# Score products of an RWKV-7 layer: two heads in turn, chunk by chunk, into two PSUM banks

## The chip, the core and the metric

The kernel runs as one program on one core of a Trainium2 chip. The metric is the device time of one execution in microseconds (us). The core has five instruction streams that run side by side and meet at semaphores: TensorE (PE) for matrix products, VectorE (DVE), ScalarE (ACT) and GpSimd (POOL) for element-wise work, and SyncE (SP), which issues most of the DMAs. PE writes its results to PSUM, which has eight banks of 128 partitions by 512 fp32 values here; the other engines take them from there.

## The reference

Two decoder layers over one sequence of 256 tokens with model width 1024. Layer 0 mixes tokens by RWKV-7 (16 heads of 64), layer 1 by block attention; each mixer is followed by a SwiGLU feed-forward part, and each sub-layer by a residual and a LayerNorm. The part that matters here, for every head of layer 0:

```python
r, k, v = einsum(...)            # three projections of the shifted input
w = -softplus(-(w0 + tanh(xw @ w1) @ w2)) - 0.5
a = sigmoid(a0 + (xa @ a1) @ a2)
g = sigmoid(xg @ g1) @ g2        # the gate, applied at the end
...
# one state S (64 x 64) per head, carried over the tokens:
# decayed by exp(-exp(w)), corrected along the normalised key, fed with k and v, read with r
```

The kernel doesn't walk over the tokens one by one. It cuts the 256 tokens into four chunks of 64, computes inside each chunk all products of keys and receptances (the scores), masks them, inverts the triangular matrix that the correction gives, and carries the state only from chunk to chunk.

## The kernel before

Layer 0's mixer takes the first 236 us, its feed-forward part follows, then layer 1. Within the mixer the stages are these. Names are those of the tiles, as the rows show them.

- **Projections.** k, r and v; weights are split into a high and a low part (ACT casts `hi`, DVE or POOL subtracts to get `lo`). The v products are issued where the planner finds room.
- **Operands of the scores.** For each of four quads q (two pairs of heads each; index j is the pair, hp the head of a pair, which sits in partitions 0 to 63 or 64 to 127) `KB[q]` holds the scaled keys and `AR[q]` the correction vectors and receptances. Generators `weigh(q)` and `keys(q)` write `KB`; `weigh` has waits of the form `yield I.idle("DVE")`, so the planner lets it go on only when, by its model, DVE has little queued.
- **Scores** (`scores(q)`, the function of the change). For each pair and head four products of 64x128 by 128 columns, one per chunk, fill one bank `sc`. `done`, one DVE multiplication of the bank by the causal mask, writes it to `SC`. There are 16 banks in all.
- **Transposes of KB** (`bkt`), the `bonus` sums from `rk`, products of the gate (`g<-mix`, then `hg`, then `g<-hg`).
- **Inverse** (`inverse`). Four DVE transposes `LT`, 31 steps of multiply (`tmp`) and add (`TT`) on DVE, each waiting for the last one, two transposes `TN`, and four transposes back into `SC`. It starts when all four quads of `SC` are there.
- **Merge** (`merge`). Products of 32x32: four groups `n` (16 each), copied by ACT into `TN`, then four groups `t`, copied by ACT into `SC`.
- **Recurrence** (`recurrence`). For four chunks and two halves f of the heads: products `z`, `u`, `s`, `y`, with copies between them. Calls of `fill` between the steps let other products (v, then the output projection o) in.
- **Tail.** Transposes `yt`, normalisation and gate, output projection `o`, residual, LayerNorm (`xtok`), then the feed-forward part begins (`gn`, `gu`).

What sets the order of the instructions: the generators are handed to `Issue` with a rank (scores has 4, `done` has 0, lower goes first). `Issue.run` keeps a modelled clock for each engine (`Clock.charge`), always resumes the ready generator of lowest rank, and so fixes one order of instructions for each engine before the kernel runs. On the chip each engine follows its order strictly; an instruction that waits holds up everything behind it on that engine. All instructions are recorded under one line, L300, that of the helper that issues them, so the rows tell them apart by tile names alone.

In `scores` the planner gets control back at each `yield 0.0`, and at each `I.after` a `done` is registered that it may place as soon as the bank is modelled as ready:

```python
I.after(ps, done, j, hp, ps)
yield 0.0
```

Of the kernel before, what the change touches and what calls it, by code (L numbers as in the profile page):

```python
# [23 lines left out]
NC = T // C  # L24
# [5 lines left out]
HALF = (slice(0, 64), slice(64, 128))  # L30
# [392 lines left out]
def trunk(ctx, tc, a, out):  # L423
# [16 lines left out]
    def nm(s):  # L440
        uid[0] += 1
        return f"{s}{uid[0]}"

    def bank(name):
        return pp.tile([128, 512], F32, tag="ps", name=nm(name))

    def slot(shape, name, dtype=F32):
        return tp.tile([128] + shape, dtype, tag="t4", name=nm(name))
# [7 lines left out]
    I = Issue(clk)  # L456
    E = {}

    def ev(name):
        return E.setdefault(name, Event())  # L460
# [9 lines left out]
    def mm(ps, lhsT, rhs, start, stop, **kw):  # L470
        pe.matmul(ps, lhsT, rhs, start=start, stop=stop, **kw)
# [21 lines left out]
    for u in range(4):  # L493
        q, o = u // 2, (u % 2) * 2
# [35 lines left out]
    def count(n, fn):  # L530

        left = [n]

        def call():
            left[0] -= 1
            if left[0] == 0:
                fn()
        return call
# [231 lines left out]
    AR = [slot([2, NC, 2, C], "AR") for _ in range(4)]  # L770
# [68 lines left out]
    KB = [slot([2, NC, 2, C], "KB") for _ in range(4)]  # L839
# [36 lines left out]
    def scores(q):  # L876

        yield ev(f"kb{q}")
        yield ev(f"ar{q}")
        yield ev("SC")  # L880
        fin = count(4, lambda: I.reach(ev(f"sc{q}"), SC[:, :, q * 2:q * 2 + 2]))

        def done(j, hp, ps):
            dve.tensor_tensor(SC[:, hp, q * 2 + j], ps.rearrange("p (c t) -> p c t", c=NC),
                              mask[:, None, :].to_broadcast([128, NC, 128]), ALU.mult)
            fin()

        for j in range(2):
            for hp in range(2):
                rs = HALF[hp]  # L890
                ps = bank("sc")
                for c in range(NC):
                    mm(ps[:, c * 128:(c + 1) * 128], KB[q][rs, j, c].rearrange("p o t -> p (o t)"),
                       AR[q][rs, j, c].rearrange("p o t -> p (o t)"), True, True)
                I.after(ps, done, j, hp, ps)
                yield 0.0

    def transposed(q):

# [779 lines left out]
    for q in range(4):  # L1679
        I.add(2, keys(q), True)  # L1680
        I.add(4, scores(q))
        I.add(5, transposed(q))
# [92 lines left out]
```

## Time and profile before

| | |
|---|---|
| median of 3 runs | 750.04 us (747.36 to 753.28) |
| the profiled execution's own time | 746.08 us |
| its span, first to last instruction | 744.3 us |
| busy PE, DVE, ACT, POOL | 93%, 73%, 51%, 25% of the span |
| mean granted TensorE clock | 0.959 of full speed |
| mixer of layer 0 | 0 to 236 us |
| first score product, last score bank masked | 84.6 us, 102.3 us |
| steps of the inverse | 108.6 to 140.7 us |
| recurrence, first u to last y | 164.5 to 195.5 us |

The span is the time from the first to the last instruction of the profiled execution; 1.8 us of its own time lie outside. The profiled execution is one of the quicker ones: 4 us under the median. Shares of busy time are averages over the whole program: PE is the fullest engine over the span, but between 70 and 140 us it is DVE that has no gaps. The granted clock is the share of full speed at which TensorE was allowed to run in a stretch: 1.00 is its upper level of 2.4 GHz, 0.50 the lower one of 1.2 GHz.

### The profile page before, as it was taken

The page shows a single profiled execution, that of the slowest core. Times are in us where ns is not written, and L with a number is a line of the kernel's source. Part 1 is how long each engine was busy: PE and PEld are TensorE (multiplying, and loading weights), DVE is VectorE, ACT ScalarE, POOL GpSimd, SP SyncE. Part 2 cuts the span into 40 slices and gives each one's busy share as a digit, 9 for nine tenths or more (in the row PEclk, how much of TensorE's full clock was granted, in tenths as well). Part 3 has the DMA queues.
Part 4 walks back from the last instruction along what each step waited for, and adds up shares of the span by engine and source line. Part 5 has one row for each costly group of instructions (what it writes and reads, how often), then busy time and mean ns, then how long its engine had stood idle before and what let it go on. Part 6 is the DMA issues. An engine that isn't in the chain of part 4 may idle for free.

```text
span 744.3 us, 11759 instructions
## 1 busy us (share of the span) xinstructions
PE 689.4 (93%) x4500; PEld 587.6 (79%) x4500; DVE 539.7 (73%) x915; ACT 382.2 (51%) x679; POOL 185.0 (25%) x132
## 2 busy tenths in 40 slices
PE   6899795998889999999999699999979999999995
PEld 5799684777678888888888488777769888888885
DVE  7989999948897766656657935977776665666576
ACT  5974134456545554554556324756635545545550
POOL 5777964343463000000001613113040000000000
PEclk9999898779899999999999889999989999999999
DMA  6445312120565655655557615345046556555551
GB/s 242 152 147 187 107 57 86 57 83 7 188 223 172 227 178 190 196 183 187 197 182 240 201 34 182 125 142 199 28 170 195 178 194 197 175 194 192 187 160 56
DMA packets 33576, 117.21 MB, mean 157 GB/s; under 512 B 3808, under 2 KB 4832, under 8 KB 33520
## 3 DMA queue, kind: packets, MB, share of 16 engines
q1 hardware_dynamic: 31936, 110.89, 44.6%
q10 hardware_dynamic: 1584, 5.57, 2.5%
q8 instruction: 35, 0.57, 0.3%
q14 instruction: 21, 0.17, 0.1%
HBM read 115.40 MB, written 1.05 MB: 156 GB/s over the span
## 4 chain that ended last, share of the span: by engine, by line
PE 68%; DVE 8%; ACT 2%; DMA 2%; issue 1%; DVEq 0%; ACTq 0%
PE gu L300 29%; PE acc L300 14%; PE qkv L300 9%; PE o L300 5%; DVE xtok L300 3%; PE gn L300 2%; PE v L300 1%; PE tr L300 1%; DMA raw<-in_w_qkv_dram 1%; DVE sc L300 1%; PE ptr L300 1%; PE pv L300 1%; PE n L300 1%; ACT hi L300 1%; PE att L300 1%
## 5 line engine op out<-in xcount | busy, mean ns | idle before, releaser
L300 DVE TENSOR_TENSOR lo<-raw,hi 128x1024 fp32r<-128x1024 f32 (+1 forms) x172 | 210.3, 1228 | 144.6 <-ACT hi L300 144.4
L300 ACT CAST hi<-raw 128x1024 fp32r<-128x1024 f32 (+1 forms) x214 | 212.0, 999 | 186.2 <-issue 93.1
L300 PE MATMUL gu<-xw,hi 128*128 128x512 f32 x640 | 226.1, 395 | 0.0
L300 PE MATMUL gu<-xw,lo 128*128 128x256 f32 x640 | 179.8, 281 | 0.0
L300 POOL TENSOR_TENSOR lo<-raw,hi 128x1024 fp32r<-128x1024 f32 (+1 forms) x41 | 87.8, 2158 | 261.3 <-ACT hi L300 257.6
L300 PEld LDWEIGHTS gu<-xw,hi 128*128 128x128 f32 x640 | 120.3, 188 | 27.1
L300 PEld LDWEIGHTS gu<-xw,lo 128*128 128x128 f32 x640 | 120.9, 189 | 0.7
L300 PE MATMUL acc<-hi,hl 128*128 128x512 f32 (+1 forms) x180 | 53.8, 369 | 0.0
L300 PE MATMUL acc<-lo,hh 128*128 128x512 f32 (+1 forms) x180 | 53.7, 368 | 0.0
L300 PE MATMUL acc<-hi,hh 128*128 128x512 f32 (+1 forms) x180 | 53.5, 366 | 0.0
L300 PE MATMUL qkv<-hi,xhi 128*128 128x512 f32 x96 | 40.7, 424 | 2.3 <-ACT xhi L300 2.3
L300 PE MATMUL qkv<-hi,xlo 128*128 128x512 f32 x96 | 39.3, 409 | 0.0
L300 ACT ACTIVATE silu<-silu 128x256 f32<-128x256 f32 x40 | 16.7, 417 | 44.0 <-DVE silu L300 44.0
L300 PE MATMUL qkv<-lo,xhi 128*128 128x512 f32 x96 | 39.0, 406 | 0.0
L300 PEld LDWEIGHTS acc<-hi,hl 128*128 128x128 f32 x180 | 32.8, 188 | 6.2
L300 PEld LDWEIGHTS acc<-lo,hh 128*128 128x128 f32 x180 | 32.7, 188 | 5.6
L300 PEld LDWEIGHTS acc<-hi,hh 128*128 128x128 f32 x180 | 31.8, 188 | 6.0
L300 PE MATMUL o<-hi,xhi 128*128 128x512 f32 x64 | 28.6, 447 | 3.0 <-ACT xhi L300 3.0
L300 PE MATMUL o<-lo,xhi 128*128 128x512 f32 x64 | 27.5, 430 | 0.0
L300 PE MATMUL o<-hi,xlo 128*128 128x512 f32 x64 | 27.3, 429 | 0.0
L300 POOL TENSOR_TENSOR ro<-ro 128x512 f32<-128x512 f32 x8 | 12.1, 1515 | 57.1 <-DVE ro L300 57.1
L300 PE MATMUL gn<-hi,xw 128*128 128x256 f32 x128 | 24.4, 287 | 0.4 <-ACT xw L300 0.3
(227 smaller groups left out, 1292.5 us busy)
## 6 DMA issues: line engine op xcount, KB each, us to landing
raw<-in_w_in_dram SPq DMA_DIRECT2D x80, 512.0 KB, 3.3
raw<-in_w_dn_dram SPq DMA_DIRECT2D x44, 512.0 KB, 3.3
raw<-in_w_qkv_dram SPq DMA_DIRECT2D x24, 512.0 KB, 3.4
raw<-in_w_o_dram SPq DMA_DIRECT2D x20, 512.0 KB, 3.5
raw<-in_w_r_dram SPq DMA_DIRECT2D x8, 512.0 KB, 3.4
raw<-in_w_v_dram SPq DMA_DIRECT2D x8, 512.0 KB, 3.3
raw<-in_w_if_dram SPq DMA_DIRECT2D x8, 512.0 KB, 3.6
raw<-in_w_k_dram SPq DMA_DIRECT2D x6, 512.0 KB, 3.8
```

What stands on the lines that cost most here:

```text
L300: ins = f(*args, **kw).ins
```

## The change

The two heads of a pair get a bank each at once. The products are then issued chunk by chunk, head 0 and head 1 in turn, so that neighbouring products read different halves of the partitions and write different banks. Both `done` calls are registered when the pair's eight products are issued, and the generator gives control back to the planner once for each pair, not once for each head. The arithmetic, the number of products and the number of banks are as before.

```diff
         for j in range(2):
+            ps = [bank("sc") for _ in HALF]
+            for c in range(NC):
+                for hp, rs in enumerate(HALF):
+                    mm(ps[hp][:, c * 128:(c + 1) * 128], KB[q][rs, j, c].rearrange("p o t -> p (o t)"),
+                       AR[q][rs, j, c].rearrange("p o t -> p (o t)"), True, True)
             for hp in range(2):
-                rs = HALF[hp]
-                ps = bank("sc")
-                for c in range(NC):
-                    mm(ps[:, c * 128:(c + 1) * 128], KB[q][rs, j, c].rearrange("p o t -> p (o t)"),
-                       AR[q][rs, j, c].rearrange("p o t -> p (o t)"), True, True)
-                I.after(ps, done, j, hp, ps)
-                yield 0.0
+                I.after(ps[hp], done, j, hp, ps[hp])
+            yield 0.0
```

Since the planner gets control back at other points of its modelled clock, the order of the other work moves too, on PE, DVE, ACT and POOL, from the scores up to the start of the feed-forward part. SP's order stays the same. Three places follow; numbers behind the names are buffers and differ between the two programs.

**PE, around the scores of the last quad (q = 3).** `sc` are score products, `bkt` transposes of KB, `v` products of the value projection; KB_133 and AR_123 are the operands of quad 3. Before:

```order
L300 MATMUL sc_1025<-AR_122,KB_132 128x128 x4
L300 MATMUL bkt_1033<-cst,KB_130 128x128 x4
...
L300 MATMUL bkt_1069<-cst,KB_132 128x128 x4
L300 MATMUL sc_1075<-AR_123,KB_133 128x128 x4
L300 MATMUL sc_1081<-AR_123,KB_133 128x128 x4
L300 MATMUL sc_1087<-AR_123,KB_133 128x128 x4
L300 MATMUL sc_1093<-AR_123,KB_133 128x128 x4
L300 MATMUL bonus_169<-selrk,rk_1023 128x2 x4
L300 MATMUL v_1106<-hi_831,xhi_865 128x512
```

With the change:

```order
L300 MATMUL sc_1013<-AR_122,KB_132 128x128
L300 MATMUL bkt_1026<-cst,KB_130 128x128 x4
...
L300 MATMUL bkt_1058<-cst,KB_132 128x128 x4
L300 MATMUL v_1067<-hi_831,xhi_865 128x512
L300 MATMUL v_1067<-lo_832,xhi_865 128x512
...
L300 MATMUL bonus_169<-selrk,rk_1108 128x2 x4
...
L300 MATMUL v_1068<-hi_912,xlo_868 128x512
L300 MATMUL sc_1151<-AR_123,KB_133 128x128
L300 MATMUL sc_1152<-AR_123,KB_133 128x128
```

Between the last `bkt` of quad 2 and the first `sc` of quad 3 there now stand 36 v products and all four bonus groups; before there stood nothing. The other 12 v products of this half follow the scores.

**DVE, from the operands of the scores to the inverse.** The rows of DVE's order, before:

```order
L300 TENSOR_TENSOR AR_122<-r_799,G_114 128x8x64
L300 TENSOR_TENSOR KB_133<-k_117,E_112 64x8x64 x2
L300 TENSOR_TENSOR KB_133<-kkr_119,a_110 64x8x64
L300 TENSOR_TENSOR AR_123<-r_869,G_114 128x8x64
L300 TENSOR_TENSOR SC<-sc_945,cst 128x512
L300 TENSOR_TENSOR rk_1045<-r_701,k_116 128x512
...
L300 TENSOR_TENSOR SC<-sc_1087,cst 128x512
L300 STREAM_TRANSPOSE LT_165<-SC 32x32x32
L300 TENSOR_TENSOR SC<-sc_1093,cst 128x512
L300 STREAM_TRANSPOSE LT_165<-SC 32x32x32 x3
```

With the change:

```order
L300 TENSOR_TENSOR rk_1102<-r_799,k_117 128x512
L300 TENSOR_TENSOR AR_123<-r_869,G_114 128x8x64
L300 TENSOR_TENSOR rk_1108<-r_869,k_117 128x512
L300 TENSOR_TENSOR SC<-sc_945,cst 128x512
...
L300 TENSOR_TENSOR SC<-sc_1013,cst 128x512
L300 TENSOR_TENSOR KB_133<-k_117,E_112 64x8x64 x2
L300 TENSOR_TENSOR KB_133<-kkr_119,a_110 64x8x64
L300 TENSOR_TENSOR SC<-sc_1151,cst 128x512
L300 TENSOR_TENSOR SC<-sc_1152,cst 128x512
L300 TENSOR_TENSOR SC<-sc_1162,cst 128x512
L300 TENSOR_TENSOR SC<-sc_1163,cst 128x512
L300 STREAM_TRANSPOSE LT_165<-SC 32x32x32 x4
```

The operands KB_133 of quad 3 were made before the first score bank was masked; they now come behind twelve masked banks (quads 0 to 2), and all four LT transposes come behind the last bank.

**PE, the merge.** `n` and `t` are the groups of 32x32 products, `v` the products of the second half of the value projection. Before, the differences of PE's order show 29 of these 48 v products among n, t, z and u, as here:

```order
L300 MATMUL n_1425<-TN_167,SC 32x32 x16
L300 MATMUL n_1426<-TN_167,SC 32x32 x16
L300 MATMUL v_1437<-lo_1400,xhi_867 128x512
L300 MATMUL v_1437<-hi_1399,xlo_868 128x512
L300 MATMUL n_1425<-TN_167,SC 32x32 x16
L300 MATMUL v_1437<-hi_1399,xhi_867 128x512
L300 MATMUL n_1426<-TN_167,SC 32x32 x16
```

With the change:

```order
L300 MATMUL v_1467<-hi_1347,xlo_868 128x512
L300 MATMUL n_1480<-TN_167,SC 32x32 x16
L300 MATMUL n_1481<-TN_167,SC 32x32 x16
L300 MATMUL n_1480<-TN_167,SC 32x32 x16
L300 MATMUL n_1481<-TN_167,SC 32x32 x16
L300 MATMUL t_1482<-SC,TN_167 32x32 x16
L300 MATMUL t_1483<-SC,TN_167 32x32 x16
L300 MATMUL z_1651<-UV_137,SC 64x64 x8
```

All 48 now stand ahead of the first n, and no v stands in the merge or behind it. In the same way the 12 output products o and the transposes `yt` that stood inside the recurrence stand behind the last y, and two pairs of `lo` (lo_1387, lo_1409) and the eight copies `AZ` on POOL, most of which followed the inverse, now stand in one run ahead of POOL's `gT`. One DVE pair, lo_1363, stands inside the inverse.

## Rows read from the trace of the kernel before

**Rows 1.** Windows view, by stage: length, busy time (instructions) per engine, clock, DMA.

```profile
108.50:140.70 32.20, 23.65 (x107) 19.81 (x106) 31.45 (x110) 15.37 (x27) 12.30 (x8) 0.84 0.20 66
...
236.10:392.00 155.90, 155.89 (x844) 134.36 (x844) 96.35 (x133) 81.56 (x133) 2.40 (x1) 1.00 0.57 189
```

**Rows 2.** Timeline of PE, scores: start, duration, operation, count, idle before and releaser.

```profile
84.64 3.68 PE L300 MATMUL sc<-AR,KB 64*128 64x128 f32 x40
88.66 4.65 PE L300 MATMUL sc<-AR,KB 64*128 64x128 f32 x56 [0.34 <-DVE SC L300]
...
96.33 2.92 PE L300 MATMUL sc<-AR,KB 64*128 64x128 f32 x32
```

**Rows 3.** Timeline of DVE, from the score operands to the inverse's first step.

```profile
82.78 2.85 DVE L300 TENSOR_TENSOR KB<-k,E 64x512 f32<-64x512 f32 x2
...
87.84 0.67 DVE L300 TENSOR_TENSOR SC<-sc,cst 128x512 f32<-128x512 f32 x1
...
93.82 3.06 DVE L300 TENSOR_TENSOR SC<-sc,cst 128x512 f32<-128x512 f32 x5
97.53 1.95 DVE L300 TENSOR_TENSOR SC<-sc,cst 128x512 f32<-128x512 f32 x3 [0.65 <-PE sc L300]
...
102.33 6.12 DVE L300 STREAM_TRANSPOSE LT<-SC 32x1024 f32<-32x1024 f32 x3
108.56 0.19 DVE L300 TENSOR_TENSOR tmp<-LT,TT 128x31 f32<-128x31 f32 x1
```

**Rows 4.** Timeline of PE in layer 1: products that already alternate between heads.

```profile
466.23 1.58 PE L300 MATMUL att<-kT,qT 64*128 64x128 f32 x16
```

**Rows 5.** Timeline of PE: bonus, first of 36 v, gate products.

```profile
104.75 1.84 PE L300 MATMUL bonus<-selrk,rk 128*128 128x2 f32 x16
106.46 0.48 PE L300 MATMUL v<-hi,xhi 128*128 128x512 f32 x1
...
114.90 7.07 PE L300 MATMUL g<-mix,nat 128*128 128x256 f32 x32
```

**Rows 6.** Timeline of DVE: inverse, first and last of five long places, transposes behind.

```profile
110.71 0.30 DVE L300 TENSOR_TENSOR tmp<-LT,TT 128x135 f32<-128x135 f32 x1
111.04 2.39 DVE L300 TENSOR_TENSOR TT<-TT,tmp 128x135 f32<-128x135 f32 x1
...
138.19 2.46 DVE L300 TENSOR_TENSOR TT<-TT,tmp 128x16 f32<-128x16 f32 x2
140.74 3.96 DVE L300 STREAM_TRANSPOSE TN<-TT 32x1024 f32<-32x1024 f32 x2
144.73 7.93 DVE L300 STREAM_TRANSPOSE SC<-TT 32x1024 f32<-32x1024 f32 x4
```

**Rows 7.** Timeline of POOL beside the inverse.

```profile
110.75 2.52 POOL L300 TENSOR_TENSOR hi<-raw,hi 32x1024 fp32r<-32x1024 f32 x1 [2.24 <-ACT hi L300]
...
138.12 4.77 POOL L300 TENSOR_TENSOR lo<-raw,hi 128x1024 fp32r<-128x1024 f32 x2 [16.73 <-ACT hi L300]
142.96 1.95 POOL L300 COPY AZ<-AR 64x384 f32<-64x384 f32 x4
```

**Rows 8.** Timeline of PE: merge, first u, first output product after the recurrence.

```profile
142.83 2.21 PE L300 MATMUL n<-TN,SC 32*32 32x32 f32 x64 [0.60 <-DVE TN L300]
...
147.48 1.91 PE L300 MATMUL n<-TN,SC 32*32 32x32 f32 x32
...
164.46 0.51 PE L300 MATMUL u<-zs,SC 64*64 64x64 f32 x10
...
199.06 0.80 PE L300 MATMUL o<-hi,xhi 128*128 128x512 f32 x1 [2.99 <-ACT xhi L300]
```

**Rows 9.** Windows view: before the merge, in it, and in the recurrence.

```profile
136.51:146.75 10.24, 9.12 (x121) 7.15 (x120) 10.05 (x21) 5.76 (x10) 6.68 (x6) 1.00 0.32 104
146.75:153.58 6.83, 6.83 (x46) 5.46 (x44) 5.86 (x3) 3.50 (x8) 1.04 (x1) 0.50 0.00 0
171.16:186.83 15.67, 13.39 (x317) 11.54 (x317) 14.88 (x56) 8.57 (x20) 3.90 (x5) 1.00 0.01 4
```

## The prediction

> **What bounds the kernel now.** Read the stage windows first. In the stretch from 108.5 to 140.7 us DVE is busy 31.45 of 32.20 us while PE is busy 23.65: a serial chain on DVE sets the time there. In the first feed-forward part PE is busy 155.89 of 155.90 us [rows 1]; that part starts when the mixer's last outputs are there, so whatever the mixer gains or loses up to 236 us comes out at the end one to one. The question is only what the change does inside the mixer.
>
> Next the two timelines of the score stretch. PE computes banks in runs of 40, 56 and 32 instructions, eight to a bank, and one of them waits for DVE to clear a bank [rows 2]. DVE masks a bank in 3.06/5 = 0.61 us and waits for PE once, 0.65 us [rows 3]. So DVE sets the pace of the scores. Then DVE goes on without a gap: four LT transposes (three in 6.12, 2.04 us each), first step of the inverse at 108.56 [rows 3], last step done and TN begun at 140.74 [rows 6], merge, and the first u of the recurrence at 164.46 [rows 8]. The recurrence ends at about 195.5 us, the output products start at 199.06 [rows 8].
>
> **What the change does, part by part.**
>
> *The products themselves.* The run of 56 takes 4.58 us for 7 banks, 0.65 each; the run of 32 takes 2.86 us to the next product, 0.72 each [rows 2]. The attention products of layer 1, which alternate already, are the nearest price for the new order: their 16 instructions, half of them twice as wide, do the columns of three banks in 1.58 us, 0.53 each [rows 4]. PE gains between nothing and 0.2 us a bank, 3 us over 16 banks at most. I book zero: DVE masks no bank faster than 0.61, and 12 of the 16 banks queue up for it. The Trainium skill, "TensorEngine Tiling (Array Packing)", section PSUM Bottleneck, speaks against the change in the same way: tiling quickens TensorE and not the emptying of PSUM, which may become the bottleneck. Rows 3 agree, with 0.61 us for emptying a bank. If PE's pace counted instead, the sum would be up to 3 us lower.
>
> *Scores of quad 3 come later.* This is the large term. DVE: AR_122 ends at 82.78 [rows 3]. Two rk (0.60 each, as a bank), AR_123 once the last r product is there (PE starts its scores at 84.64 [rows 2]), a third rk, so the first mask starts near 86.1, not 87.84 [rows 3]. Twelve masks at 0.60 end at 93.3. PE meanwhile has done quads 0 to 2 and the bkt; the v products need banks that the last masks set free, so they start near 93.4. The 36 v cost (114.90 - 106.46)/36 = 0.234 us each, 8.4 in all; two bonus groups cost 1.71, so four cost 3.4 [rows 5]. Quad 3's scores start at about 105.2 (now 96.33 [rows 2]). Two banks at 0.53 and the way to DVE: first mask 106.3, fourth done 108.8. Then four LT in a row, 8.2 us, where now one of them lies in the wait for the last bank. First step of the inverse at 117.0 instead of 108.56: **+8.5 us**. DVE stands idle some 11 us in between, about 95 to 106. KB_133, put behind twelve masks, would be done by 95.2 and is not what delays quad 3; the v products are. I give this term 7 to 10.
>
> *The inverse itself.* Of its 32.2 us, 9.8 are five places where a step that would take a third of a microsecond takes over two: 0.30 for 135 elements, then 2.39 for as many, exactly beside a POOL operation of 2.52 that starts just before it; at the end 2.46 beside two lo [rows 6, 7]. Undisturbed it is 22.4. With the change POOL's mix, three of the lo, the hi and the first pair of v run from about 96 to 116, into DVE's idle time, and no longer hit. Two full lo still do (their casts on ACT stand behind the gate's copies): 4.2 to 4.9. Then a v (0.7), DVE's own two lo_1363 (1.2, new here), two pairs of smaller lo, a second v and eight AZ copies, all now ahead of the inverse's end. Each pair costs 2.3 if it hits as rows 6 show, nothing if it falls on a transpose; the AZ copies, 0.49 each [rows 7], cost 0 to 4. I take 4.8 for these. 117.05 + 22.4 + 4.2 + 0.7 + 1.2 + 4.8 = 150.3: TN begins 9.6 later than 140.74 instead of 8.5: **+1.1 us** (-2.5 to +4.5).
>
> The Trainium skill, "SBUF — State Buffer", section "SBUF: two separate sides", has a rule for such blocking: DVE with two SBUF inputs and a GpSimd operation that reads SBUF lock each other out for the whole instruction. Rows 6 and 7 agree for TENSOR_TENSOR; for COPY on POOL no row here shows it. By that rule the copies block too, and this term would be 4 us higher than with copies that are free.
>
> *From TN to the first u.* Now 23.7 us (140.74 to 164.46). DVE's six transposes take 11.9 of it [rows 6], a floor for the first u. Beyond that PE has 29 v products among the eight groups. Without them: 2.1 us to the first n, eight groups, some 2 us of ACT copies. A group is 1.1 us at the full clock (two in 2.21) and 1.84 at half (1.91 less the overlap with the next) [rows 8]: 12.5 to 13 or 18.8 us. Which clock? In the trace PE entered the merge at 1.00 after dense v products and fell to 0.50 after 4 us of n and few v [rows 9]. With the change the gate's products follow hg at about 125 and take some 5 us, the 48 v 11.2 more: they end near 142, and PE idles some 8 us before the first n. So I take half: **-4.9 us** (-11.2 at full clock).
>
> *Recurrence.* The 12 o and four v go out of it (16 x 0.234 = 3.7), and yt, for whose input PE waits; of PE's 2.28 us of idle time from 171.16 to 186.83 [rows 9] I take 1.4 back with it: -5.1. From 171.16 to 186.83 the recurrence holds the full clock with neither v nor o in it [rows 9], so it can live without them; starting from half it loses 2 to 4 until the clock is back. I take 3.5: **-1.6 us** (-5 to +2).
>
> *Tail.* The 12 o must still be done, 2.8 us, and yt, part of the gating and some weight splits now follow the last y. Their cover was the recurrence. **+3.2 us** (+1 to +5).
>
> SP's order and the DMAs that it issues don't move. Sum: 8.5 + 1.1 - 4.9 - 1.6 + 3.2 = **+6.3 us**: 746.1 becomes 752.4 for the profiled execution, which is 4 under the median; on the median of 750.04 about **756.3**.
>
> **Rivals.**
>
> *Faster: the merge runs at full clock.* If PE's granted clock is 1.00 at the first n, the merge costs 12.5 instead of 18.8 and the recurrence starts warm. The place is PE just before TN; it decides whether v products, held up by late lo, still run until close to 150. With few hits at the inverse's end: +8.5 - 3.2 - 11.2 - 5.1 + 2.5 = -8.5, 741.5 us. For it: v products waited for a lo at 140 in the trace too. Against it: all 48 stand ahead of n, and their last weights should be there by 135. Chance 0.12.
>
> *Slower: the clock stays down through the recurrence.* Sparse small products from 150 to 185 at 0.50, with only n, t, z, u, s, y on PE. Each of eight steps then loses about 1.2 us, +10 on the sum: 766. It decides if the clock is still 0.50 after the second u. Against it: rows 9, last line. Chance 0.2.
>
> *The delay is not real, or evens out.* If the v products of the first half start well before 93 (banks free sooner), or the planner's new order only exchanges places, gain and loss cancel: 748 to 751. Against it: on PE the order is strict, and 36 v and four bonus stand ahead of quad 3. Chance 0.2.
>
> **Numbers.** The forecast itself, with its terms in their middle, gets 0.48. A measurement of this kernel can tell about 1% (7.5 us) from no change. The forecast's own spread is 750 to 763 and straddles that bound, a little more of it inside. Faster by over 1%: 0.09 (most of the first rival). Slower by over 1%: 0.18 of the second rival and half of the forecast, 0.42. Within: 0.49. The range runs from 744 (nearly the first rival) to 768 (the second with a bit of the bounds).
>
> **What would show it.** In the new trace: the first SC mask of quad 3 at 105 to 108 us with DVE idle some 10 us before it; the inverse's first step at 116 to 118; fewer long steps at its start, some at its end, TN at 147 to 153; no v between n and t, with the clock at 0.50 there; first u 19 us after TN; no o before the last y. Wrong: quad 3's scores before 100, or a clock of 1.00 in the merge, which would bring 6 us back.

## The result and the profile after

The changed kernel takes 753.18 us (median of 20 runs, 749.89 to 756.47), the kernel before 748.88 us in the same comparison: ratio 1.0059, 95% interval 1.0037 to 1.0081. That is 4.3 us slower, under 1%. One of the 20 runs of the kernel before took 959.71 us and is left out of the ratio, which counts the runs within 1.5% of the fastest of their kernel. The prediction of 756 us within 744 to 768, with "within 1%" as its likeliest case (0.49, against 0.42 for slower by more), holds.

The profiled execution of the change took 754.6 us (span 752.8), 1.4 above its median; that of before is 2.8 under the median of this comparison. So the two traces stand 8.5 us apart, the medians 4.3, and a part of what follows is spread. The line of busy times on the page of the changed kernel:

```profile
PE 687.7 (91%) x4500; PEld 587.8 (78%) x4500; DVE 541.9 (72%) x915; ACT 381.5 (51%) x679; POOL 183.4 (24%) x132
```

It says nothing of the change, which adds and removes no product (x4500 as before). What moved is seen at waypoints, read from the timelines (start of the named instruction, us; the last five columns are experiments told below, with their numbers):

| waypoint | before | change | alternation, old order (3) | change again (2) | KB earlier (6) | o earlier (9) | block order, two banks at once (1) |
|---|---|---|---|---|---|---|---|
| DVE masks first SC | 87.84 | 85.49 | 88.12 | 86.69 | 88.65 | 85.95 | 87.86 |
| last mask ends | 102.30 | 108.04 | 100.15 | 109.42 | 101.21 | 108.53 | 102.32 |
| inverse, first step | 108.56 | 116.31 | 108.51 | 117.70 | 109.69 | 116.80 | 108.57 |
| TN begins | 140.74 | 152.57 | 143.49 | 153.85 | 139.78 | 152.94 | 143.25 |
| first u | 164.46 | 170.14 | 171.06 | 171.42 | 168.62 | 170.51 | 168.09 |
| last y ends | 195.49 | 197.87 | 202.05 | 198.58 | 202.81 | 207.33 | 200.40 |
| feed-forward part starts | 241.03 | 250.42 | 247.87 | 248.69 | 252.06 | 251.43 | 245.92 |

**The scores.** Timeline of DVE with the change, beside [rows 3] (start, duration, instruction, count, idle before and its releaser):

```profile
85.49 7.25 DVE L300 TENSOR_TENSOR SC<-sc,cst 128x512 f32<-128x512 f32 x12
92.66 1.79 DVE L300 TENSOR_TENSOR KB<-k,E 64x512 f32<-64x512 f32 x2
94.48 0.68 DVE L300 TENSOR_TENSOR KB<-kkr,a 64x512 f32<-64x512 f32 x1
105.56 2.48 DVE L300 TENSOR_TENSOR SC<-sc,cst 128x512 f32<-128x512 f32 x4 [10.40 <-PE sc L300]
108.07 8.13 DVE L300 STREAM_TRANSPOSE LT<-SC 32x1024 f32<-32x1024 f32 x4
116.31 0.19 DVE L300 TENSOR_TENSOR tmp<-LT,TT 128x31 f32<-128x31 f32 x1
```

Twelve masks run without a gap at 7.25/12 = 0.60 us a bank, as fast as before and no faster. KB_133 is done at 95.16, and then DVE stands idle 10.40 us for quad 3. PE in the same stretch, beside [rows 2], and through the merge, beside [rows 8]:

```profile
83.96 5.63 PE L300 MATMUL sc<-AR,KB 64*128 64x128 f32 x96
89.52 2.84 PE L300 MATMUL bkt<-cst,KB 128*128 128x128 f32 x24
92.28 0.47 PE L300 MATMUL v<-hi,xhi 128*128 128x512 f32 x1
...
104.37 2.06 PE L300 MATMUL sc<-AR,KB 64*128 64x128 f32 x32
...
154.50 6.68 PE L300 MATMUL n<-TN,SC 32*32 32x32 f32 x125 [13.73 <-DVE TN L300]
...
170.14 0.80 PE L300 MATMUL u<-zs,SC 64*64 64x64 f32 x10
```

Alternated, twelve banks take 5.63 us, 0.47 each, where seven took 4.58 [rows 2]. PE is ahead of DVE by the twelfth bank and turns to v products at 92.28; quad 3's scores stand behind 36 of them and the bonus groups and start at 104.37, not 96.33.

**The inverse.** DVE at its end, beside [rows 6], and POOL at the same time, beside [rows 7]:

```profile
128.50 2.72 DVE L300 TENSOR_TENSOR tmp<-LT,TT 128x240 f32<-128x240 f32 x2
...
140.36 3.44 DVE L300 TENSOR_TENSOR lo<-raw,hi 128x512 fp32r<-128x512 f32 x2
143.73 2.33 DVE L300 TENSOR_TENSOR tmp<-LT,TT 128x128 f32<-128x128 f32 x2
...
146.62 1.01 DVE L300 TENSOR_TENSOR tmp<-LT,TT 128x112 f32<-128x112 f32 x2
...
149.10 1.00 DVE L300 TENSOR_TENSOR TT<-TT,tmp 128x96 f32<-128x96 f32 x2
150.03 0.35 DVE L300 TENSOR_TENSOR tmp<-LT,TT 128x80 f32<-128x80 f32 x2
...
152.57 3.79 DVE L300 STREAM_TRANSPOSE TN<-TT 32x1024 f32<-32x1024 f32 x2
```

```profile
128.79 4.99 POOL L300 TENSOR_TENSOR lo<-raw,hi 128x1024 fp32r<-128x1024 f32 x2 [13.55 <-ACT hi L300]
...
139.05 5.87 POOL L300 TENSOR_TENSOR lo<-raw,hi 128x512 fp32r<-128x512 f32 x4 [2.01 <-ACT hi L300]
144.89 1.08 POOL L300 TENSOR_TENSOR v<-v,sb 128x512 f32<-128x512 f32 x1
146.03 4.00 POOL L300 COPY AZ<-AR 64x384 f32<-64x384 f32 x8
```

Read the two side by side; a pair is the two instructions (x2) of one multiply or one add. While POOL works on lo, DVE's steps take up to 2.7 us a pair; while it copies AZ, from 146.03 to 150.03, pairs take 0.7 to 1.0; and the first pair that starts when POOL is done takes 0.35.

**Merge, recurrence, tail.** Windows of the change, beside [rows 1, 9] (start and end, length, then busy time and instructions of PE, PEld, DVE, ACT and POOL, granted clock, DMA):

```profile
116.30:152.60 36.30, 19.38 (x85) 15.52 (x83) 35.65 (x113) 15.68 (x32) 16.95 (x16) 0.79 0.20 72
...
152.00:164.00 12.00, 9.50 (x185) 9.50 (x186) 11.81 (x11) 3.39 (x6) 0.00 (x0) 0.50 0.01 3
164.00:174.60 10.60, 10.60 (x155) 9.34 (x153) 3.51 (x11) 4.77 (x10) 1.60 (x2) 0.50 0.01 2
174.60:197.90 23.30, 21.43 (x517) 18.59 (x515) 20.59 (x72) 11.60 (x30) 5.00 (x7) 0.99 0.08 26
```

All v products are out before 140.8, PE then does nothing for 13.7 us, the granted clock falls, and the whole merge and the first 4 us of the recurrence run at 0.50, though PE works without a gap from 154.5 on; from 174.6 on it is 0.99. Waits of PE behind the last y, from 197.9 to 250.5 us (total, times, longest):

```profile
PE o L300 <- ACT xhi L300: 2.8, 1, 2.8
PE gn L300 <- ACT xw L300: 2.7, 2, 2.5
PE yt L300 <- DVE y L300: 1.3, 1, 1.3
PE o L300 <- DVE xlo L300: 1.1, 1, 1.1
```

Before, the first of these was there too (2.99, [rows 8]), and gn waited for xw for 0.3 us; yt and xlo are new here: yt and the gating have come out of the recurrence.

### The profile page after: what moved, and what is told of

Its sections match the earlier page's. It is cut to its first block, busy times and chain, and to the rows that moved or that the text cites. A ratio compares the mean times of both kernels' runs of the same rounds, so it can differ in the third digit from the quotient of the medians.

```text
span 752.8 us, 11767 instructions
## 1 busy us (share of the span) xinstructions
PE 687.7 (91%) x4500; PEld 587.8 (78%) x4500; DVE 541.9 (72%) x915; ACT 381.5 (51%) x679; POOL 183.4 (24%) x132
## 4 chain that ended last, share of the span: by engine, by line
PE 66%; DVE 23%; ACT 4%; DMA 3%; issue 3%; SPq 0%; DVEq 0%; ACTq 0%
PE gu L300 28%; PE acc L300 13%; PE qkv L300 9%; DVE xtok L300 4%; DVE lo L300 3%; PE gn L300 2%; DVE tmp L300 2%; DVE TT L300 2%; PE o L300 2%; DMA raw<-in_w_dn_dram 1%; PE r L300 1%; ACT hi L300 1%; PE v L300 1%; PE tr L300 1%; PE k L300 1%
## 5 line engine op out<-in xcount | busy, mean ns | idle before, releaser
L300 DVE TENSOR_TENSOR lo<-raw,hi 128x1024 fp32r<-128x1024 f32 (+1 forms) x172 | 216.0, 1260 | 146.0 <-ACT hi L300 145.6
L300 POOL TENSOR_TENSOR lo<-raw,hi 128x1024 fp32r<-128x1024 f32 (+1 forms) x41 | 88.9, 2186 | 252.4 <-ACT hi L300 250.5
L300 PE MATMUL o<-hi,xhi 128*128 128x512 f32 x64 | 27.7, 433 | 2.8 <-ACT xhi L300 2.8
```

What stands on the lines that cost most here:

```text
L300: ins = f(*args, **kw).ins
```

## The experiments

Edits are shown against the changed kernel, unless said otherwise. Each ratio is to the kernel before, timed on the same chip.

**1. Is it the two banks at once and the single hand-over, or the alternation?** The products of a pair go head by head again; all else is as changed.

```diff
-            for c in range(NC):
-                for hp, rs in enumerate(HALF):
+            for hp, rs in enumerate(HALF):
+                for c in range(NC):
```

> The two banks of a pair are taken at once and control goes back to the planner once a pair, as in the change, but the products stay head by head. The order of all engines comes out as before. If the loss comes from the order in which the other work stands (my theory), the time is that of the kernel before, ratio 0.997 to 1.003, the inverse's first step at 108 to 109 us. If two banks at once or the coarser hand-over cost something by themselves, the ratio is near that of the change, 1.006.

750.05 us, 1.0038 (1.0005 to 1.0070). The ratio lies just above the 0.997 to 1.003 that was expected (the medians are 750.05 and 748.41 us). The instructions stand in the order of before on every engine, and the inverse's first step is at 108.57 (before 108.56, [rows 3]):

```profile
97.55 1.95 DVE L300 TENSOR_TENSOR SC<-sc,cst 128x512 f32<-128x512 f32 x3 [0.65 <-PE sc L300]
...
108.57 0.19 DVE L300 TENSOR_TENSOR tmp<-LT,TT 128x31 f32<-128x31 f32 x1
```

It has two uses. The hand-over is not what moves the order; the alternation is. And it is the order of before once more, yet its TN begins 2.5 us later and its ratio is 1.0038: what is under some 0.4% here can't be put down to a change, and waypoints from TN on spread by several us. The inverse's first step, by contrast, is there to 0.01 us (with the change it spreads by 1.4, experiment 2).

Its POOL and DVE at the end of the inverse show where the 2.5 us come from:

```profile
137.67 4.80 POOL L300 TENSOR_TENSOR lo<-raw,hi 128x1024 fp32r<-128x1024 f32 x2 [16.26 <-ACT hi L300]
```

```profile
137.75 2.48 DVE L300 TENSOR_TENSOR TT<-TT,tmp 128x32 f32<-128x32 f32 x2
140.17 2.44 DVE L300 TENSOR_TENSOR tmp<-LT,TT 128x16 f32<-128x16 f32 x2
```

POOL's last two lo start 0.45 us earlier than before (138.12, [rows 7]), so both meet a step with two inputs. Before, only the first did (2.46 us, [rows 6]); the second fell beside TN's transposes. The inverse of the same order takes 34.7 us here and 32.2 before.

**2. The same, from the other side.** Alternation, with the two hand-overs of before:

```diff
             for hp in range(2):
                 I.after(ps[hp], done, j, hp, ps[hp])
-            yield 0.0
+                yield 0.0
```

> The change with control handed back to the planner twice a pair, as before the change; products alternate and both masks are registered behind the pair's last product. The order and the waits of all engines come out exactly as with the change, so this is the change a second time. If the order is all that counts: median 751 to 755, the inverse's first step at 116 to 117, TN at 151 to 154, first u at 168 to 172. If the number of hand-overs counted by itself, the first step would lie nearer 108.6.

754.67 us, 1.0082 (1.0048 to 1.0116). The order is that of the change; first step 117.70 (116 to 117 was expected), TN 153.85, feed-forward part 248.69. With experiment 1 this corrects the account of the change above: it is not that the planner gets control back at other points. In alternating order both banks of a pair have their last product at the end of the eight, so by the planner's model the first bank is ready later; experiment 3 bears this out, as products charged as in block order bring nearly the old order back.

**3. Alternation alone.** The products alternate, but the planner charges them as it did before (head 0 at once, head 1 behind the hand-over), which gives nearly the old order. `prods` lists the operands of the products; while `clk.mute` is set the planner's clock isn't charged:

```diff
...
+                for hp in range(2):
+                    clk.mute = hp == 1
+                    mm(*prods[c][hp])
+            clk.mute = False
+            I.after(ps[0], done, j, 0, ps[0])
+            yield 0.0
+            for c in range(NC):
+                x = prods[c][1]
+                clk.charge("PE", "matmul", x[:3], dict(start=True, stop=True))
+            I.after(ps[1], done, j, 1, ps[1])
             yield 0.0
```

> The products alternate between the heads, but the planner is charged as if they came head by head, so the other work keeps nearly the order of before (KB of quad 3 ahead of the first mask, quad 3's scores ahead of the v products). Theory: alternation gains PE some 2 us in the score stretch, all of it hidden behind the masks on DVE: ratio 0.996 to 1.002, masks still 0.60 us apart, inverse's first step within 1.5 us of 108.6. Rival, that alternating products are themselves slower or that the change's loss is theirs: ratio 1.004 or more. Rival, that PE's gain shows in the end: 0.995 or less.

751.17 us, 1.0048 (1.0026 to 1.0070). Its DVE:

```profile
97.66 2.48 DVE L300 TENSOR_TENSOR SC<-sc,cst 128x512 f32<-128x512 f32 x4 [1.10 <-PE sc L300]
100.18 8.23 DVE L300 STREAM_TRANSPOSE LT<-SC 32x1024 f32<-32x1024 f32 x4
108.51 0.19 DVE L300 TENSOR_TENSOR tmp<-LT,TT 128x31 f32<-128x31 f32 x1
```

The last mask ends at 100.15 instead of 102.30, but the inverse starts at 108.51, where it did. Before, one LT stood in the wait for the last bank [rows 3]; here all four come behind it. What PE saves comes out as nothing at the first step, as the prediction booked it.

The whole time does not bear this out as expected: 1.0048 lies not in 0.996 to 1.002 but where the rival stood (1.004 or more, the loss is that of the products themselves). Experiment 1, which moves nothing at all, is at 1.0038 in the same set of runs, and the medians of the two are 1.1 us apart. So the times decide neither for the order nor for the rival; against the rival speak the first step, which is not later, and the price of the products in experiments 4 and 5.

**4 and 5. No wait for KB_133.** The other guess at why quad 3 is late: its operands. The generator makes KB_133 without waiting for an idle DVE, with the change and without it.

```diff
-        yield I.idle("DVE")
+        if u < 3:
+            yield I.idle("DVE")
```

(at its three places)

> The change with one edit: the generator that makes the keys of quad 3 no longer waits for a modelled idle DVE, so KB of quad 3 stands ahead of the masks and quad 3's scores ahead of the v products again. Theory: the 10 us in which DVE waits for quad 3 vanish; masks from about 85.5 to 95.2 us, four LT, the inverse's first step near 103.5 to 105 (108.6 before, 116.3 with the change). The inverse then meets more of POOL's lo again, so TN at 134 to 139 (140.7 before); ratio to the kernel before 0.990 to 0.998. If the v products or POOL are what delays the inverse anyway, the first step stays at 108 or later and the ratio is at 1.0 or above.

> The same edit on the kernel before, products head by head. Theory: masks are paced by DVE in both, so this one is within 0.3% of the change with the same edit, if the rest of the order is as good; ratio to before 0.990 to 1.000. If alternation is needed to feed DVE, its masks are 0.65 to 0.7 us apart, not 0.60, and the inverse starts 1 to 2 us later than in the other.

753.18 us, 1.0042 (1.0009 to 1.0074), and 751.31 us, 1.0039 (1.0011 to 1.0067). The two are within 0.3% of each other, as expected, but neither is under 1.000, and the first step came at 109.92 and 109.25, not at the 103.5 to 105 expected of the change. The miss is an instruction that I had not followed: KB_133 now stands ahead of the lo of the r weights on DVE, and r waits for it until 85.52, where before it waited until 79.44. PE with the change:

```profile
85.52 0.58 PE L300 MATMUL r<-xhi,lo 128*128 128x256 f32 x1 [6.19 <-DVE lo L300]
...
90.57 7.42 PE L300 MATMUL sc<-AR,KB 64*128 64x128 f32 x128
```

and in block order:

```profile
89.33 9.59 PE L300 MATMUL sc<-AR,KB 64*128 64x128 f32 x128
```

By accident this is the cleanest price of the alternation: 16 banks in one run, at a granted clock of 1.00 and 0.99, take 7.42 us against 9.59, 0.46 and 0.60 each. DVE masks all 16 in 9.65 us in the first: its pace is the slower one there and no faster than PE's in block order, and the 2.2 us never reach the path.

**6. KB_133 behind AR_122.** So that r is not held up, KB_133 waits for AR_122 to be made:

```diff
-        yield I.idle("DVE")
+        yield ev("ar2") if u == 3 else I.idle("DVE")
```

> The change with one edit: the generator of quad 3's keys waits for AR of quad 2, not for a modelled idle DVE, so KB of quad 3 stands where it stood before, ahead of the first mask, and quad 3's scores ahead of all 48 v products. The products still alternate. Theory: the delay of the scores (7.7 us at the inverse's first step) is that one move: first step back at 107.5 to 109.5, TN at 139 to 144, time within 0.4% of before. Rival, that alternation delays the scores in another way: first step at 112 or later, ratio 1.006 or more.

The waypoints came as expected: first step 109.69, TN 139.78, both within 1.2 us of the kernel before. The time did not (within 0.4% was expected): 754.54 us, 1.0060 (1.0026 to 1.0094), the change's own. PE behind TN:

```profile
141.78 3.00 PE L300 MATMUL n<-TN,SC 32*32 32x32 f32 x64 [2.05 <-DVE TN L300]
144.71 0.80 PE L300 MATMUL v<-hi,xhi 128*128 128x512 f32 x1
...
147.57 3.62 PE L300 MATMUL n<-TN,SC 32*32 32x32 f32 x64
```

The v products are between the groups again, and from TN to the first u it takes 28.8 us, where the change needs 17.6. It is more than the 23.7 before, and the reason stands in the order: between the first n and the first u there are 45 of the 48 v products, where the kernel before has 26 and the change none. The gate's products, which stand ahead of them, wait for hg until 131.04 and once more until 135.37. So this edit brings the first step back and not the order behind it; what it gives back at the scores it spends in the merge. It shows that an early first step alone isn't worth its 7.7 us. What the time would be with the first step early and the merge as before, it doesn't show.

**7. Do POOL's copies hold up the inverse?** Each AZ copy is replaced with a fill of the same tile, which reads nothing; the copying is left out. The planner is still charged a copy, so the order is the change's.

```diff
-            pool.tensor_copy(out=AZ[q][ur, :, hp, 1:], in_=AR[q][vr, :, 1:, 0, :])
+            clk.mute = True
+            pool.memset(AZ[q][ur, :, hp, 1:], 0.0)
+            clk.mute = False
+            clk.charge("POOL", "tensor_copy", (), dict(out=AZ[q][ur, :, hp, 1:], in_=AR[q][vr, :, 1:, 0, :]))
```

> The change with POOL's eight AZ copies replaced by fills with zero, which read no SBUF; the order is the same, and the copying of AR into AZ is left out of the computation. Theory: a POOL copy blocks DVE's two-input steps like POOL's subtractions do, so the last steps of the inverse, which took 0.7 to 1.0 us beside the copies, fall to 0.35 to 0.5 and TN comes 2 to 3 us earlier, at 149 to 150.6, the time 1 to 3 us lower than the change's. Rival, that only POOL operations with two inputs block: TN stays within 0.7 us of 152.6.

POOL and DVE at the end of the inverse:

```profile
145.82 3.03 POOL L300 MEMSET AZ<- 64x384 f32 x8
```

```profile
146.91 0.40 DVE L300 TENSOR_TENSOR tmp<-LT,TT 128x112 f32<-128x112 f32 x2
...
150.69 1.88 DVE L300 STREAM_TRANSPOSE TN<-TT 32x1024 f32<-32x1024 f32 x1
```

The pair that took 1.01 beside the copies takes 0.40 beside the fills. The inverse takes 33.7 us where the change took 36.3 and 36.2 (experiment 2): the copies cost 2.5. Experiment 11, where ACT does the copies and nothing is left out, has 33.7 too. The Trainium skill, "SBUF — State Buffer", section "SBUF: two separate sides", has a lock between a DVE operation with two SBUF inputs and a GpSimd operation that reads SBUF; by that rule a copy blocks and a fill does not, and this experiment agrees for both. The whole kernel: 752.59 us, 1.0048 (1.0016 to 1.0080), not to be told from the change.

**8. Is the half clock in the merge worth anything?** 80 dense products of no use are put ahead of n, to fill PE's idle time.

```diff
+        if hp == 0:
+            clk.mute, clk.ordered, x = True, True, mixed["xv"][0][0]
+            for _ in range(80):
+                mm(tps[0], x[:, 0, 0:128], x[:, 0:2, :].rearrange("p a t -> p (a t)"), True, True)
+            clk.mute = clk.ordered = False
```

> The change with 80 more dense products (128x512, results overwritten) on PE just ahead of the merge, in the time in which PE idles; 12 to 18 v products then fall into the merge and the first step of the recurrence. Theory: PE enters the merge at a granted clock of 1.00, the first n groups cost 1.1 us, not 1.7 to 1.9; with some v back in the merge TN to first u takes 14 to 18 us (17.6 with the change, 23.7 before), and the recurrence starts at 1.00, so first u to last y takes 25 to 27 (27.7). Time 1 to 5 us lower than the change's. Rival, that idle time before the merge is not what sets the clock in it: clock 0.50 in n and t all the same, and no gain.

762.19 us, 1.0174 (1.0136 to 1.0211): a miss, and not a clean test. Its windows:

```profile
127.00:154.90 27.90, 26.13 (x115) 20.70 (x113) 27.71 (x78) 7.93 (x15) 8.55 (x7) 1.00 0.17 57
154.90:160.00 5.10, 3.13 (x69) 2.62 (x69) 3.31 (x2) 1.69 (x4) 1.01 (x2) 1.00 0.00 0
160.00:177.60 17.60, 17.60 (x223) 14.95 (x223) 0.32 (x2) 7.47 (x14) 5.99 (x6) 0.51 0.20 61
```

```profile
136.65 18.32 PE L300 MATMUL t<-xhi 128*128 128x512 f32 x80
154.90 2.21 PE L300 MATMUL n<-TN,SC 32*32 32x32 f32 x64
```

The dense run lasted 18.32 us. TN had begun at 145.80 (the four smaller lo of POOL and seven of its eight AZ copies no longer stood inside the inverse, which took 28.8 us), so n started some 7 us later than it could have, and v products came back between the groups. The clock stayed at 1.00 to 160.0, so dense work ahead of the merge does hold it; but behind two groups of n (32 instructions each), three v and 2 us of waiting for ACT it was 0.51 all the same. The warm start gave back two groups (2.21 us for both), not the merge.

**9 to 11. Bring the o products back.** The group norm of the first 128 tokens is put first (rank 0, no wait for an idle DVE), so that output products run in the recurrence: with the change, with the kernel before, and with the change and the AZ copies on ACT.

```diff
-            yield I.idle("DVE")
+            if hf == 1:
+                yield I.idle("DVE")
...
-            I.add(7, group_norm(hf, f))
+            I.add(0 if hf == 0 else 7, group_norm(hf, f))
```

and for the last also

```diff
-            pool.tensor_copy(out=AZ[q][ur, :, hp, 1:], in_=AR[q][vr, :, 1:, 0, :])
+            act.copy(out=AZ[q][ur, :, hp, 1:], in_=AR[q][vr, :, 1:, 0, :])
```

> The change with the normalisation of the first 128 tokens given rank 0 (7 in the change) and freed of its waits for a modelled idle DVE, so that 24 output products o stand inside the recurrence again (12 before, none with the change). Theory: what the change loses in the end is the tail, 50 to 52.5 us from the last y to the first gu against 45.5 before, by 12 more o and by output weights that are asked for later. Then the tail falls to 40 to 46, the recurrence grows by 2 to 6, and the time is 2 to 8 us under the change's: 746 to 751, ratio to before 0.996 to 1.003. Rival, that the loss is the late inverse: it starts at 116 to 118 here too, so the time stays at 752 to 756, ratio 1.005 or more.

> The same edit on the kernel before (30 o inside the recurrence, 12 before). If the tail's length is worth what I think, this too gains 2 to 5 us, ratio 0.993 to 0.999, and the difference between this and the change with the same edit is within 3 us. If the tail is paced by something else (DVE, the weights' DMAs), the ratio is 0.999 to 1.003.

> The change with the normalisation first and POOL's eight AZ copies put on ACT, which also lets them stand behind the transposes in the order. Theory: TN comes 2 to 3 us earlier than in the change (149.5 to 151 against 152.6), ACT has room for 4 us of copies in the merge if they don't delay its TN and SC copies; the time is 0 to 3 us under that of the version with normalisation first alone. If ACT's copies in the merge are in the way, u comes later and the gain is gone.

756.19 us, 1.0116 (1.0075 to 1.0157); 757.70, 1.0109 (1.0066 to 1.0152); 759.90, 1.0142 (1.0100 to 1.0183). All three miss what was expected of them: 746 to 751 us, a ratio of 0.993 to 0.999, and up to 3 us under the first of them. 1.0116 is where the rival of the late inverse stood, but the kernel before with the same edit, whose inverse starts at 108.24, is as slow. Recurrence and tail as windows, first with the change and the norm first, then of the change:

```profile
170.51:207.33 36.82, 32.49 (x606) 27.14 (x605) 28.49 (x91) 15.25 (x38) 9.58 (x10) 0.96 0.24 86
207.33:251.43 44.10, 35.08 (x196) 28.47 (x195) 37.77 (x80) 22.05 (x40) 21.34 (x12) 0.96 0.54 167
```

```profile
170.14:197.87 27.73, 25.86 (x574) 22.33 (x574) 23.25 (x81) 12.50 (x33) 6.57 (x8) 0.91 0.07 22
197.87:250.42 52.55, 43.10 (x226) 35.38 (x227) 45.07 (x90) 24.61 (x44) 24.81 (x15) 0.94 0.56 190
```

The tail falls by 8.5 us as hoped, and the recurrence grows by 9.1: with 25 o products in it PE is busy 6.6 us longer, and it waits 2.5 longer. In the kernel before, too, the tail falls (45.5 to 43.7) and the recurrence grows (31.0 to 40.4). With the copies on ACT, TN comes 2.4 us earlier than with them on POOL (150.50 against 152.94), as expected; the end does not.

## Why the prediction was right, and where its terms were off

It was right in kind: the alternation makes PE faster where PE is not what is waited for, and its real effect is an order of work that moves time from one place to another. By its terms (us), from the two profiled executions, and beside them the same two orders a second time, experiment 2 less experiment 1:

| term | forecast | change less before | experiment 2 less 1 |
|---|---|---|---|
| the products | 0 | 0 (experiments 3, 4, 5) | |
| scores later, first step | +8.5 | +7.75 | +9.1 |
| inverse | +1.1 (-2.5 to +4.5) | +4.1 (36.3 less 32.2) | +1.5 (36.2 less 34.7) |
| TN to first u | -4.9 (-11.2 at full clock) | -6.2 (17.6 less 23.7) | -7.3 |
| recurrence | -1.6 (-5 to +2) | -3.3 (27.7 less 31.0) | -5.2 |
| tail | +3.2 (+1 to +5) | +7.0 | +4.6 |
| behind it | 0 | -0.9 | +2.2 |
| sum | +6.3 | +8.5 | +5.0 |

By medians it is +4.3. The signs of the five terms are right both times. That the sum comes close is in part luck: the tail and the inverse were booked too low, the saving between TN and the last y too low as well (6.5, against 9.5 and 12.4), and these errors partly cancel. "Within 1%" is no proof either: the order of before against itself (experiment 1) falls within 1% as well, so the time alone could not have told a right mechanism from a wrong one. What bears the mechanism out is the waypoints.

**The products.** PE's gain turned out at the upper half of the bound (0.14 us a bank in experiments 4 and 5, under 0.2), and zero was right for the reason given, DVE's 0.60 us a bank.

**Scores later.** The cause holds in each step: masks from 85.49, KB_133 done at 95.16, 36 v and the bonus groups ahead of quad 3 on PE, DVE idle 10.40 us. Quad 3 began 0.8 us earlier than worked out: v could start at 92.28, as PE needed no bank that the twelfth mask sets free. The term repeats (experiment 2: 117.70; experiment 9: 116.80), and goes when KB_133 is made earlier (experiment 6): the planner then sees quad 3's operands ready and puts its scores first. So the forecast's sentence that KB_133 "is not what delays quad 3" holds for the chip, where PE had v ahead of it in its queue, but KB_133 is what made the planner queue them so.

**The inverse** with the change was mis-sized: 36.3 us, where 33.3 was forecast. Most of the 3.0 is DVE's own two lo_1363. They were booked at 1.2, their undisturbed time (1.28 in experiment 8, where POOL is idle then); they took 3.44, beside POOL's four lo. A two-input DVE operation newly put there is itself blocked. The AZ copies, allowed 0 to 4 within the 4.8 for lo, v and copies, cost 2.5 (experiment 7). Experiment 8 fits this: with the four lo and seven of the eight copies out of it, the inverse took 28.8. But what the term is as a difference depends on the execution of before: the change's inverse repeats (36.3, 36.2, and 36.1 in experiment 9), that of the old order takes 32.2 or 34.7, as half a microsecond on POOL decides (experiment 1).

**TN to first u.** Half clock and no v, as forecast; 17.6 us instead of 18.8. The n started 1.9 us after TN, and from there to the first u it took 15.6. Two readings of the forecast were slightly off, with little effect on a sum: of the 29 v it places among the groups, 26 stand between the first n and the first u and three behind it (it takes four out of the recurrence); and by its own times PE would idle 10 us before the first n, not 8 (13.7 measured).

**Recurrence.** The clock was back at about 175, inside the second of its steps, and the stretch behind it ran at 0.99 without v and o: the gain was twice what I took, and in experiments 2 and 1 as large as the bound of -5.

**Tail.** Direction right, size uncertain. PE is busy 43.10 us in it instead of 39.90, which is the +3.2 forecast for the o and yt; the other 3.8 are time without work for PE, in which the waits for xlo, y and xw are new or longer. Those were not in the sum. But experiment 6, where the 12 o are back in the recurrence, has a tail of 49.3 too, and experiment 1, the program of before, 45.5. So +4.6 to +7 is what these traces show; how much of it is the change's and how much an execution's own clock and waits is open.

**The rivals.** *Faster, by a full clock in the merge* did not happen: the clock was 0.50 from 152 on. Experiment 8 says that its condition would not have been enough either, as the clock was 0.51 again 5 us behind the first n. *Slower, by half the clock through the recurrence* did not happen: it ended at about 175, in time. *The delay evens out* was wrong in that the delay is real (116.31) and half right in the sum: of the 11.8 us by which TN is late, 9.5 are won back by the last y. The medians are 4.3 us apart and the two traces 8.5; the difference is the 2.8 by which the one execution lies under its median and the 1.4 by which the other lies above.

**What stays open.** A difference of 0.59% stands beside 0.38% for the order of before timed against the kernel before, whose interval (1.0005 to 1.0070) lies above 1 as well. That the change is not faster is shown, and so is that the alternation, by way of the planner, delays the scores. Two sets of runs (1.0059 and 1.0082) say that it is slower, but how much of this is the change's and not the comparison's own error is open, and so is which of the terms makes the loss: experiment 3 has nearly the old order and 1.0048. None of the eleven versions beat the kernel before.

## What to carry to other kernels

A quicker engine is worth its waiters' time and no more: masks at 0.60 us a bank swallow products at 0.46. Where a planner sets the order, an edit of four lines is priced by the order that comes out, and work that is taken out of one serial stretch (the v, the o) is looked for in the next one before it is booked as a gain. When moving a delay back leaves the time unchanged, as in experiment 6, count what stands in the stretches behind it: there the 45 v in the merge had eaten the gain. And run the old order a second time before a waypoint's shift is put down to an edit: half a microsecond on POOL moved TN by 2.5 (experiment 1).

## What the runs showed of the hardware

- 64-row products of 128 columns that alternate between the halves and two banks take 0.46 us for a bank (eight instructions), 0.60 in block order (7.42 and 9.59 us for 128, experiments 4 and 5).
- Beside POOL copies that read SBUF, DVE's two-input pairs took 0.7 to 1.0 us, beside fills 0.40; with the lo on POOL up to 2.7 in the change. DVE's transposes took 1.98 us each beside POOL's lo and copies [rows 6, 7], and 1.90 with the change, where POOL is idle.
- 18.3 us of dense products held the granted clock at 1.00 for 5 us more, in which two groups of 32x32 products, three v and a wait of 2 us stood; it was then 0.51 (experiment 8). With the change it was 0.50 from 154.5 to 174.6, while PE worked without a gap through small products, most of them 32x32 and 64x64.
- Two executions of the same order were 2.5 us apart at TN and 3.6 at the first u, while the inverse's first step repeated to 0.01 us (before and experiment 1; the two traces of the change differ by 1.4 there).
